# A two-layer decoder trunk on one core: smaller GpSimd pieces, a shorter group norm and a new order of the work between the chains of the RWKV scan

## The chip, the core and the metric

The kernel runs on one core of a Trainium2 chip. Its engines run side by side, each through its own fixed row of instructions, and wait for each other by semaphores: TensorE (PE in the profile; PEld is its loading of weights), VectorE (DVE), ScalarE (ACT), GpSimd (POOL) and SyncE (SP), which issues the transfers. The metric is the device time of one execution in microseconds, less being better.

## What is computed

Layer 0 has stick-breaking attention and a pooling mixer, layer 1 an RWKV-7 time mixing; a layer norm follows each. The sequence has 512 tokens, the model 2048 channels, all in float32. The change lies in layer 1. Its heart is a recurrence for each of 32 heads of 64 channels, followed by a group norm per head and a gate:

```
def step(state, inp):
    r_t, w_t, k_t, v_t, kk_t, a_t = inp
    sa = einsum('bhvk,bhk->bhv', state, -kk_t)
    state = state * w_t + sa[..., None] * (kk_t * a_t) + v_t[..., None] * k_t
    return state, einsum('bhvk,bhk->bhv', state, r_t)
...
mean = jnp.mean(o, axis=-1, keepdims=True)
var = jnp.mean(jnp.square(o - mean), axis=-1, keepdims=True)
o = ((o - mean) * lax.rsqrt(var + GN_EPS)).reshape(B_, S, D) * gn_w + gn_b
bonus = jnp.sum(r * k * r_k, axis=-1, keepdims=True) * v
o = (o + bonus.reshape(B_, S, D)) * jax.nn.silu(g)
return o @ w_o
```

## The kernel before

Matrix products are made in split precision: `split` (L135) writes a float32 tile as a high part (a cast on ACT, L137) and a low part (a subtraction, L138, on DVE, or on GpSimd where the caller says so), and `mm3` (L140) makes three matmuls of the parts. Layer 0, the projections of layer 1 (k, r, g) and the output projection are such products and are not touched.

`scan` (L827) takes the 32 heads in 16 pairs. For a pair the 512 tokens are cut into 8 chunks of 64, and within a chunk the recurrence is written as small matrix products. These functions make the parts of a pair:

- `vproj` (L857): the projection v, 16 blocks of 3 matmuls (L142 to L144, tile `vps`) in split precision. The weights come in units of four blocks; from the third pair on the low part of a unit, 128 x 512, is one GpSimd subtraction (`wlo`, L138).
- `gprod` (L876): loads the pair's factors, makes the products `g` of keys and queries in two halves (L890), masks them on DVE into `Z` (L896), and transposes the keys into `BT` (L902, L903). Each half of `g` takes two PSUM banks of the pool `pa`, which has two buffers and also serves the transpositions.
- `vprep` (L906): the bonus term `bv` on GpSimd (L911) and v by token (`RS`, L918 to L921).
- `lanes` (L926): the inverse of the diagonal blocks of 16, on DVE. Four GpSimd instructions gather the blocks (`nd`, L931), DVE transposes them (`lt`, L936), then 15 steps of one product `pr` and one sum `uc` each follow (L943, L944). It ends in `U` (L958).
- `levels` (L962): joins the blocks of 16 to 64 by four products on PE: `q1`, `c1` (added into `U` on DVE, L994, and transposed into `UT`, L996), `q2` (which reads `UT`) and `c2` (added into `U`, L1007).
- `chain` (L1010): the recurrence over the chunks, in three steps a chunk. In the first, PE makes `xo` (L1025 with the state `M`, L1028), and DVE and ACT copy it to `xs` (L1032, L1033). In the second, PE makes `sa` from `xs` and `U` (L1036), and DVE copies it to `RS` (L1037). In the third, PE makes `s1` from `RS` (L1043), DVE updates `M` (L1052, L1054), PE completes `xo` (L1057) and ACT copies it to `O` (L1060).
- `post` (L1064): the group norm of the pair's `O` on DVE and ACT (L1072 to L1083, with `rsqrt_eps`, L201), its transposition `ot` on PE (L1087), bonus and gate.

The order of PE's instructions is the order of the code; those of the other engines are put in a row by the scheduler, the chains' first. The main loop (from L1208) makes rounds of 12 slots. In a round two chains go one step a slot each: the second half of pair p's (the older one) and the first half of pair p+1's (the younger one). So slots 0, 3, 6 and 9 hold first steps, 1, 4, 7 and 10 second steps, and 2, 5, 8 and 11 third steps. Behind the two chains' step a slot holds what fills PE until the next one. `plan` (L1144) gives each visit of a generator a due time, spread evenly over an interval of slots, and `slot` (L1148) takes visits in the order of their due times. The intervals stand in L31 and L32, counted from the beginning of the round two before the one in which the pair's chain starts: `GP` for gprod, `VJ` for vproj, `LA` for lanes, `LV` for levels, `VP` for vprep, and `PO` for post. From pair 13 on, units of the output projection's weights and its first matmuls (`y`) fill in.

Of the kernel before, what the change touches and what calls it, by code (L numbers as in the profile page):

```python
# [8 lines left out]
F32 = mybir.dt.float32  # L9
# [20 lines left out]

PO, LA, VP, LV, GP, VJ = (13.5, 20), (8, 15), (21.5, 25), (16, 24.5), (0.5, 9), (5.5, 17)  # L31
Q14, A13, B13, A14, B14, A15, B15, Q15 = (0, 3), (0.5, 5.5), (6, 12), (0, 10), (3, 12), (0, 9), (0.5, 11.5), (0, 11.5)  # L32


class Kernel:
# [98 lines left out]

    def split(self, hi, lo, src, eng=None):  # L135

        self.nc.scalar.copy(hi, src)  # L137
        (eng or self.nc.vector).tensor_sub(lo, src, hi.bitcast(F32))  # L138

# [60 lines left out]

    def rsqrt_eps(self, pool, v, eps, n, name):  # L201
# [5 lines left out]
        nc.vector.tensor_scalar(hx, v, eps, -0.5, ALU.add, ALU.mult)  # L207
        nc.vector.reciprocal(sd, sd)
# [618 lines left out]
    def scan(self, ctx, xv, first, mp, ld, ar_d, bk_d, bc_d, g_d, m_d):  # L827
# [29 lines left out]
        def vproj(p):  # L857
# [18 lines left out]
        def gprod(p):  # L876
# [5 lines left out]
            nc.sync.dma_start(BK.rearrange("p a b -> p (a b)"), bk_d[p])  # L882
            yield

            Z = s["Z"] = [st.tile([P, 8, P], F32, tag=f"Z{h}", name=f"Z{h}", bufs=4) for h in range(2)]
            for b in range(2):
# [10 lines left out]
                yield  # L897
            BT = s["BT"] = st.tile([P, 8, P], F32, tag="BT", name="BT")
            for b in range(2):
                g = aux("bt")  # L900
                for c in range(4):
                    nc.tensor.transpose(g[:, c * P:(c + 1) * P], BK[:, 4 * b + c, :], self.ident)  # L902
                nc.scalar.copy(BT[:, 4 * b:4 * b + 4, :], g.rearrange("p (c n) -> p c n", c=4))  # L903
                yield

        def vprep(p):  # L906
# [3 lines left out]
            nc.sync.dma_start(bv, bc_d[p])  # L910
            nc.gpsimd.tensor_mul(bv, s["vT"], bv)  # L911

# [151 lines left out]
        def post(p):  # L1064
# [7 lines left out]
            nc.vector.tensor_reduce(sm, O, AX.X, ALU.add)  # L1072
            nc.vector.tensor_scalar(sm, sm, 1.0 / 64, None, ALU.mult)
# [6 lines left out]
            nc.vector.tensor_scalar(sm, sm, 1.0 / 64, None, ALU.mult)  # L1080
            rs = self.rsqrt_eps(tp, sm, GN_EPS, 8, "gn")
            yield
# [23 lines left out]
        def units(*ks):  # L1106
            for k in ks:
                tag = "AR,Z0,Z1,AR,Z0,Z1,BT,RS,AR,Z0,Z1,BT,RS,BK,AR,Z0".split(",")[k]
                pool = ld if tag in ("AR", "BK") else st
                w = pool.tile([P, 2, S], F32R, tag=tag, name="wo", bufs=1 if k == 13 else 4 if tag[-1] in "R01" and tag != "RS" else 3)  # L1110
                raw = self.wp.tile([P, S], F32, tag="wraw", name="wraw", bufs=3)
# [47 lines left out]
        def hurry(g):  # L1159
            while True:  # L1160
# [3 lines left out]
                yield  # L1164

        def plan_pair(base, q, skip=0):

            gp = gprod(q)
            next(gp)
            plan(base, gp, 6, *GP)  # L1170
            plan(base, hurry(lanes(q)) if q == 15 else lanes(q), 18, *LA)
            plan(base, hurry(levels(q)) if q == 15 else levels(q), 5, *LV)
# [6 lines left out]
        for q in range(3):  # L1179
            next(v)  # L1180
        run(gp)
        la = lanes(0)
        for q in range(16):
            next(la)
            if q % 2:
                next(v, None)
        g1, v = gprod(1), vproj(1)
        next(g1)
        run(la)
        for q in range(6):  # L1190
            next(g1)
            if q % 2:
                next(v)
        run(vprep(0))
        la, l0 = lanes(1), levels(0)
        for q in range(10):
            if q % 2 == 0:
                next(l0, None)
            if q < 6:
                next(la)  # L1200
            if q % 2:
                next(v)
        run(l0)
        plan(-12, la, 12, 12, LA[1])
        plan(-12, levels(1), 5, *LV)
        plan(-12, vprep(1), 2, *VP)
        A = None
# [111 lines left out]
```

## Time and profile before

| | |
|---|---|
| median of 3 runs | 2119.38 us (2112.89 to 2120.28) |
| the profiled execution | 2116.03 us, span 2114.3 us |
| mean granted clock of TensorE | 0.99 |
| scan: `vps` matmuls | 1401.4 to 1876.6 us |
| scan: `xo` matmuls | 1442.7 to 1942.4 us |
| `wlo` on GpSimd in the scan | 56 instructions, 74.6 us |
| `pr` (L943) of 128 x 81 on DVE | 14 instructions, mean 711 ns |

The profile is of one execution. A busy time is the union of the instructions' times on an engine; matmuls are pipelined and overlap, so a busy PE may still be waiting. In a row of the timeline stand the start, the length, the engine, the line, the operation, the tiles written and read, the shape of the array for matmuls (rows x columns), the shapes, and how many instructions are merged; in brackets stands the idle time before, with what ended it. A matmul of two float32 operands appears as two instructions. A row of the waits has the total in us, the number and the longest. In a group's row stand its busy time in us and the mean of one in ns, then the engine's idle time before it.

### The profile page before, as it was taken

How to read it: one execution, taken by the hardware profiler on the slowest of the kernel's cores; microseconds unless marked ns; L12 is line 12 of the kernel's file. 1: busy time of each engine (PE TensorE's matmuls, PEld its weight loads, DVE VectorE, ACT ScalarE, POOL GpSimd, SP SyncE). 2: the span in 40 equal slices, each digit the busy share in tenths (PEclk: the TensorE clock that was granted, in tenths of full speed). 3: DMA queues.
4: the chain of work that ended last, by engine and by line, in shares of the span. 5: the costliest groups of instructions: out<-in, count | busy, mean ns of one | idle time of the engine just before them, and what ended most of it. 6: DMA issues, size and time to landing. Idle time of an engine off the chain costs nothing. (4 is left out here: it accounts for less than half of the span.)

```text
span 2114.3 us, 33769 instructions
## 1 busy us (share of the span) xinstructions
PE 2032.7 (96%) x13139; PEld 1648.2 (78%) x13139; DVE 1295.1 (61%) x2557; ACT 956.5 (45%) x1663; POOL 250.1 (12%) x334
## 2 busy tenths in 40 slices
PE   8999999999999998999999999999999999989996
PEld 7888888888887897777788888877677676666786
DVE  5334344444433358656866776577888988886336
ACT  3345445333221138544654654455555555564211
POOL 0000000000000000233000000013333333310003
PEclk9999999999999999999999999999999999999998
DMA  5222222233333353565365556632232332232733
GB/s 192 91 79 80 80 80 65 85 95 105 100 102 117 111 176 111 157 179 173 110 210 192 197 173 217 202 120 62 91 101 81 96 106 89 85 115 95 235 105 114
DMA packets 214031, 262.97 MB, mean 124 GB/s; under 512 B 15768, under 2 KB 161776, under 8 KB 213104
## 3 DMA queue, kind: packets, MB, share of 16 engines
q1 hardware_dynamic: 213872, 260.83, 38.4%
q8 instruction: 103, 1.69, 0.3%
q14 instruction: 56, 0.46, 0.1%
HBM read 214.32 MB, written 46.47 MB: 123 GB/s over the span
## 5 line engine op out<-in xcount | busy, mean ns | idle before, releaser
L138 DVE TENSOR_TENSOR wlo<-wraw,whi 128x1024 fp32r<-128x1024 f32 (+1 forms) x268 | 313.8, 1175 | 475.9 <-ACT whi L137 464.6
L137 ACT CAST whi<-wraw 128x1024 fp32r<-128x1024 f32 (+1 forms) x324 | 302.9, 938 | 565.3 <-PE ga L143 327.0
L142 PE MATMUL ga<-mx,whi 128*128 128x512 f32 x768 | 299.9, 391 | 3.2 <-ACT mx L137 3.2
L142 PE MATMUL ga<-x,whi 128*128 128x512 f32 x768 | 300.9, 392 | 0.1
L143 PE MATMUL ga<-mx,whi 128*128 128x512 f32 x768 | 300.4, 391 | 0.0
L144 PE MATMUL ga<-mx,wlo 128*128 128x512 f32 x768 | 300.1, 391 | 0.0
L144 PE MATMUL ga<-x,wlo 128*128 128x512 f32 x768 | 299.5, 390 | 0.5 <-DVE wlo L138 0.5
L143 PE MATMUL ga<-x,whi 128*128 128x512 f32 x768 | 299.2, 390 | 0.0
L488 PE MATMUL gb<-whi,mixed 128*128 128x512 f32 (+1 forms) x576 | 198.0, 344 | 3.8 <-DVE s L439 3.8
L490 PE MATMUL gb<-wlo,mixed 128*128 128x512 f32 (+1 forms) x576 | 197.6, 344 | 3.1 <-DVE wlo L138 3.1
L489 PE MATMUL gb<-whi,mixed 128*128 128x512 f32 (+1 forms) x576 | 197.6, 343 | 0.0
L142 PEld LDWEIGHTS ga<-mx,whi 128*128 128x128 f32 x768 | 144.8, 189 | 36.1 <-ACT mx L137 3.6
L143 PEld LDWEIGHTS ga<-mx,whi 128*128 128x128 f32 x768 | 144.7, 188 | 31.5 <-DVE mx L138 0.6
L144 PEld LDWEIGHTS ga<-mx,wlo 128*128 128x128 f32 x768 | 144.8, 188 | 30.6
L144 PEld LDWEIGHTS ga<-x,wlo 128*128 128x128 f32 x768 | 144.2, 188 | 31.2 <-DVE wlo L138 1.0
L142 PEld LDWEIGHTS ga<-x,whi 128*128 128x128 f32 x768 | 144.3, 188 | 29.6 <-ACT whi L137 0.4
L143 PEld LDWEIGHTS ga<-x,whi 128*128 128x128 f32 x768 | 144.3, 188 | 29.1
L488 PEld LDWEIGHTS gb<-whi,mixed 128*128 128x128 f32 x576 | 109.8, 191 | 17.9 <-DVE s L439 5.4
L490 PEld LDWEIGHTS gb<-wlo,mixed 128*128 128x128 f32 x576 | 109.9, 191 | 16.8 <-DVE wlo L138 4.3
L489 PEld LDWEIGHTS gb<-whi,mixed 128*128 128x128 f32 x576 | 109.8, 191 | 12.4
L142 PE MATMUL vps<-mx,whi 128*128 128x512 f32 x256 | 113.8, 445 | 0.0
L138 POOL TENSOR_TENSOR wlo<-wraw,whi 128x512 fp32r<-128x512 f32 x56 | 74.6, 1332 | 257.0 <-ACT whi L137 234.8
(330 smaller groups left out, 3374.8 us busy)
## 6 DMA issues: line engine op xcount, KB each, us to landing
wraw<-in_ev_w_in SPq DMA_DIRECT2D x96, 512.0 KB, 3.6
wraw<-in_ev_w_out SPq DMA_DIRECT2D x32, 512.0 KB, 3.6
wraw<-in_od_w_k SPq DMA_DIRECT2D x32, 512.0 KB, 4.9
wraw<-in_od_w_r SPq DMA_DIRECT2D x32, 512.0 KB, 3.5
wraw<-in_od_w_g SPq DMA_DIRECT2D x32, 512.0 KB, 3.7
wraw<-in_od_w_v SPq DMA_DIRECT2D x64, 256.0 KB, 2.8
ar_d<-pAR SPq DMA_DIRECT2D x16, 512.0 KB, 2.6
bk_d<-pBK SPq DMA_DIRECT2D x16, 512.0 KB, 3.2
```

Of the source, the lines that this page charges most:

```text
L137: self.nc.scalar.copy(hi, src)
L138: (eng or self.nc.vector).tensor_sub(lo, src, hi.bitcast(F32))
L142: mm(ps, ah, bh, start=start, stop=False)
L143: mm(ps, ah, bl, start=False, stop=False)
L144: mm(ps, al, bh, start=False, stop=stop)
L488: mm(ps, ah, bh, start=start, stop=False)
L489: mm(ps, al, bh, start=False, stop=False)
L490: mm(ps, ah, bl, start=False, stop=stop)
```

## The change

The diff has three parts.

1. The GpSimd instructions of `vproj` and `vprep` are cut: the low part of a weight unit is made in four subtractions of 128 x 128, and `bv` in four products of 128 x 128.
2. In the group norm two scalings by 1/64 on DVE (L1073, L1080) are folded into their neighbours, and `hx` (L207) goes from DVE to ACT where it has eight columns.
3. `vproj` yields after each block, not after each second one. `gprod` makes `BT` ahead of `Z`, with four buffers of `BT`. The even intervals are replaced by due times of single visits (`at_`), except for post and lanes, and the interval of lanes is 4.5 to 17 where it was 8 to 15.

```diff
-PO, LA, VP, LV, GP, VJ = (13.5, 20), (8, 15), (21.5, 25), (16, 24.5), (0.5, 9), (5.5, 17)
+PO, LA = (13.5, 20), (4.5, 17)
...
-    def split(self, hi, lo, src, eng=None):
+    def split(self, hi, lo, src, eng=None, parts=1):
         self.nc.scalar.copy(hi, src)
-        (eng or self.nc.vector).tensor_sub(lo, src, hi.bitcast(F32))
+        n = src.shape[1] // parts
+        for q in range(parts):
+            sl = slice(q * n, q * n + n)
+            (eng or self.nc.vector).tensor_sub(lo[:, sl], src[:, sl], hi[:, sl].bitcast(F32))
...
-        self.split(hi, lo, raw, eng)
+        self.split(hi, lo, raw, eng, a if eng else 1)
...
-        nc.scalar.activation(sd, v, AF.Sqrt, bias=self.eps[eps])
-        nc.vector.tensor_scalar(hx, v, eps, -0.5, ALU.add, ALU.mult)
+        nc.scalar.activation(sd, v, AF.Sqrt, bias=self.eps[eps], scale=scale)
+        if n == 1:
+            nc.vector.tensor_scalar(hx, v, eps, -0.5, ALU.add, ALU.mult)
+        else:
+            nc.scalar.activation(hx, v, AF.Copy, bias=-0.5 * eps, scale=-0.5 * scale)
...
-                if k % 2 and k < NK - 1:
+                if k < NK - 1:
                     yield
...
-            nc.gpsimd.tensor_mul(bv, s["vT"], bv)
+            for q in range(4):
+                nc.gpsimd.tensor_mul(bv[:, q * P:q * P + P], s["vT"][:, q * P:q * P + P], bv[:, q * P:q * P + P])
...
-            nc.vector.tensor_scalar(sm, sm, 1.0 / 64, None, ALU.mult)
             yield
-            nc.vector.tensor_sub(O, O, bc(sm))
+            nc.vector.scalar_tensor_tensor(O, bc(sm), -1.0 / 64, O, ALU.mult, ALU.add)
...
-            nc.vector.tensor_scalar(sm, sm, 1.0 / 64, None, ALU.mult)
-            rs = self.rsqrt_eps(tp, sm, GN_EPS, 8, "gn")
+            rs = self.rsqrt_eps(tp, sm, GN_EPS, 8, "gn", 1.0 / 64)
...
+        def at_(base, g, *where):
+            todo.extend((base + x, len(todo), g) for x in where)
...
-            plan(base, gp, 6, *GP)
+            at_(base, gp, 1.6, 1.7, 3.1, 3.2, 4.1, 4.2)
...
-            plan(base, vproj(q), 8, *VJ)
-            plan(base, vprep(q), 2, *VP)
+            at_(base, vproj(q), *[x + 0.1 * n + 0.1 for x, m in ((5, 3), (7, 2), (8, 3), (11, 3), (13, 2), (14, 3)) for n in range(m)])
+            at_(base, vprep(q), 17.4, 19.5)
```

`levels` gets the due times 17.5, 18.1, 21.1, 22.1 and 24.1. In the steady rounds the work behind the chains' steps on PE is then this (v 6 stands for six matmuls of `vps`, `g` and `bt` for a half or the whole of their instructions):

| slot | step of the chains | before | after |
|---|---|---|---|
| 0 | first | a quarter of g, v 6 | c2 |
| 1 | second | a quarter of g | v 6, bt |
| 2 | third | v 6 | v 9 |
| 3 | first | a quarter of g, v 6 | half of g |
| 4 | second | a quarter of g | half of g |
| 5 | third | v 6, q1, ot | v 9, ot |
| 6 | first | half of bt, v 6 | q1 |
| 7 | second | c1, half of bt | v 6, vt |
| 8 | third | v 6 | v 9 |
| 9 | first | q2, v 6 | c1 |
| 10 | second | c2 | q2 |
| 11 | third | vt, v 6 | v 9 |

The first place is PE around the second steps of slots 7 (before) and 10 (after). Line numbers after the change are some 7 higher: L1043 is `sa`, L998 `c1`, L988 `q2` and `c2`, L1050 `s1`. Before:

```order
L1036 MATMUL sa<-xs_10939,U 64x128
L1036 MATMUL sa<-xs_10940,U 64x128
L991 MATMUL c_13649<-U,q1z 48x32 x16
L902 MATMUL bt<-ident,BK 128x128 x4
L1043 MATMUL s_13676<-RS,BT 64x64 x2
```

After, in slots 9 and 10:

```order
L998 MATMUL c_13368<-U,q1z 48x32 x16
L1043 MATMUL sa<-xs_10940,U 64x128
L1043 MATMUL sa<-xs_10939,U 64x128
L988 MATMUL q_13399<-UT,N_13242 32x32
L988 MATMUL q_13399<-UT,Z_12668 32x32
```

Before, two slots lie between `c1` and `q2`, with `s1`, `xo` and a run of `vps` in them; after, only the two `sa`. On DVE the same place after the change reads as follows (L1039 is the copy `xs`, L1044 the copy `RS`, L1001 the addition of `c1`, L1003 the transposition that `q2` reads, L950 and L951 the lanes of another pair):

```order
L1039 COPY xs_10940<-xo 64x64
L1039 COPY xs_10939<-xo 64x64
L950 TENSOR_TENSOR pr<-uc,la 128x10x10
L951 TENSOR_REDUCE uc<-pr 128x10
L1044 COPY RS<-sa 64x128 x2
L1001 TENSOR_TENSOR U<-U,c_14276 48x16x16 x2
L950 TENSOR_TENSOR pr<-uc,la 128x11x11
L1003 STREAM_TRANSPOSE UT<-U 128x256
```

Both `RS` and both additions stand ahead of `UT`.

The second place is PE in slots 0 and 1 before and 3 and 4 after, at the products `g`. Before:

```order
L890 MATMUL g<-AR,BK 128x128 x4
L142 MATMUL vps<-mx,whi 128x512
L143 MATMUL vps<-mx,whi 128x512
L144 MATMUL vps<-mx,wlo 128x512
L142 MATMUL vps<-mx,whi 128x512
L143 MATMUL vps<-mx,whi 128x512
L144 MATMUL vps<-mx,wlo 128x512
L1036 MATMUL sa<-xs_10940,U 64x128
L1036 MATMUL sa<-xs_10939,U 64x128
L890 MATMUL g<-AR,BK 128x128 x4
```

After (L903 is `g`):

```order
L903 MATMUL g<-AR,BK 128x128 x8
L1043 MATMUL sa<-xs_10939,U 64x128
L1043 MATMUL sa<-xs_10940,U 64x128
L903 MATMUL g<-AR,BK 128x128 x8
L1050 MATMUL s_13638<-RS,BT 64x64 x2
```

The two halves of `g`, which share two banks, now have only the two `sa` between them.

The third place is DVE in slots 0 and 1 after the change, where `c2` is added into `U` (L1014). The younger chain's first `sa` reads this `U`:

```order
L1039 COPY xs_10940<-xo 64x64
L1039 COPY xs_10939<-xo 64x64
L951 TENSOR_REDUCE uc<-pr 128x14
L1014 TENSOR_TENSOR U<-U,c_13925 32x8x32
L1044 COPY RS<-sa 64x128
L1014 TENSOR_TENSOR U<-U,c_13925 32x8x32
L950 TENSOR_TENSOR pr<-uc,la 128x15x15
L1085 TENSOR_REDUCE gs<-gsq 128x8
L1044 COPY RS<-sa 64x128
```

Before, the same additions (L1007) stand a slot earlier, around an update of `M`:

```order
L943 TENSOR_TENSOR pr<-uc,la 128x9x9
L1007 TENSOR_TENSOR U<-U,c_13341 32x8x32
L1052 SCALAR_TENSOR_TENSOR M_10942<-s_13360,pcs,m_13363 64x64 x2
L1007 TENSOR_TENSOR U<-U,c_13341 32x8x32
L944 TENSOR_REDUCE uc<-pr 128x9
```

The copy of the older chain's `RS` now stands between the two additions, and that of the younger behind both.

More of the change, by code (lines that the diff above doesn't have):

```diff
@@ L199, in rsqrt, with rsqrt_eps @@
         return y
-    def rsqrt_eps(self, pool, v, eps, n, name):
+    def rsqrt_eps(self, pool, v, eps, n, name, scale=1.0):
         nc = self.nc
@@ L883, in gprod @@
             yield
+            BT = s["BT"] = st.tile([P, 8, P], F32, tag="BT", name="BT", bufs=4)
+            for b in range(2):
+                g = aux("bt")
+                for c in range(4):
+                    nc.tensor.transpose(g[:, c * P:(c + 1) * P], BK[:, 4 * b + c, :], self.ident)
+                nc.scalar.copy(BT[:, 4 * b:4 * b + 4, :], g.rearrange("p (c n) -> p c n", c=4))
+                yield
             Z = s["Z"] = [st.tile([P, 8, P], F32, tag=f"Z{h}", name=f"Z{h}", bufs=4) for h in range(2)]
@@ L897, in gprod @@
                 yield
[L898 to L904, printed above, removed]
         def vprep(p):
@@ L1109, in units @@
                 pool = ld if tag in ("AR", "BK") else st
-                w = pool.tile([P, 2, S], F32R, tag=tag, name="wo", bufs=1 if k == 13 else 4 if tag[-1] in "R01" and tag != "RS" else 3)
+                w = pool.tile([P, 2, S], F32R, tag=tag, name="wo", bufs=1 if k == 13 else 3 if tag == "RS" else 4)
                 raw = self.wp.tile([P, S], F32, tag="wraw", name="wraw", bufs=3)
@@ L1184, in scan @@
             next(la)
-            if q % 2:
-                next(v, None)
+            next(v, None)
         g1, v = gprod(1), vproj(1)
@@ L1191, in scan @@
             next(g1)
-            if q % 2:
-                next(v)
+            next(v)
         run(vprep(0))
@@ L1200, in scan @@
                 next(la)
-            if q % 2:
-                next(v)
+            next(v)
         run(l0)
         plan(-12, la, 12, 12, LA[1])
-        plan(-12, levels(1), 5, *LV)
-        plan(-12, vprep(1), 2, *VP)
+        at_(-12, levels(1), 17.5, 18.1, 21.1, 22.1, 24.1)
+        at_(-12, vprep(1), 17.4, 19.5)
         A = None
```

6 lines of the change are left out of this document (3 added, 3 removed).

## The prediction, made before the changed kernel was run

> **What bounds the kernel now.** I read the page first, then the stages, then the waits inside the one stage that the diff touches, the scan (about 1,430 to 1,945 us).
>
> ```profile
> span 2114.3 us, 33769 instructions
> PE 2032.7 (96%) x13139; PEld 1648.2 (78%) x13139; DVE 1295.1 (61%) x2557; ACT 956.5 (45%) x1663; POOL 250.1 (12%) x334
> ```
> ```profile
> 1700.00:1800.00 100.00, 93.40 (x1182) 69.53 (x1178) 88.70 (x283) 55.00 (x140) 32.82 (x32) 0.98 0.35 106
> ```
>
> Columns of the stage row: length, then PE, PEld, DVE, ACT and POOL busy, then the granted clock. In the scan PE is busy 93.4 of 100 us and DVE 88.7. PE runs its instructions in one fixed row, so the scan lasts as long as PE works or waits. The chain that ended last gives the length of one pair, since the same instruction comes back in it every second pair:
>
> ```profile
> 1619.81 1.09 DVE rshgn L207
> ```
> ```profile
> 1744.32 1.09 DVE rshgn L207
> ```
>
> 124.5 us for four pairs: 31.1 us a pair of twelve slots. What PE visibly waits for in the scan:
>
> ```profile
> PE s L1043 <- DVE RS L1037: 22.9, 28, 1.7
> PE ot L1087 <- DVE O L1083: 4.0, 3, 2.8
> PE c L981 <- ACT q L1002: 2.6, 6, 1.0
> PE sa L1036 <- ACT xs L1033: 2.5, 7, 0.5
> PE xo L1025 <- DVE M L1054: 1.7, 4, 1.2
> ```
>
> One wait leads: PE's `s1` for the copy `RS`. The timeline shows where it comes from:
>
> ```profile
> 1647.81 0.17 DVE L1073 TENSOR_SCALAR gs<-gs 128x8 f32<-128x8 f32 x1
> ...
> 1650.56 1.28 POOL L138 TENSOR_TENSOR wlo<-wraw,whi 128x512 fp32r<-128x512 f32 x1 [4.06 <-ACT whi L137]
> 1650.64 1.23 DVE L1080 TENSOR_SCALAR gs<-gs 128x8 f32<-128x8 f32 x1
> ...
> 1652.82 0.66 PE L1043 MATMUL s<-RS,BT 128*64 128x64 f32 x8 [1.73 <-DVE RS L1037]
> ```
>
> The same scaling of eight numbers takes 0.17 us alone and 1.23 us beside a GpSimd subtraction that began 0.08 us before it: DVE stood still until GpSimd was done, `RS` behind it came late, and PE lost 1.73 us.
>
> **The change part by part.** The sum is made against the profiled execution, 2116.0 us (span 2114.3 and 1.7 around it), 3.4 below the median of 2119.38 and inside the runs shown.
>
> ```profile
> L138 POOL TENSOR_TENSOR wlo<-wraw,whi 128x512 fp32r<-128x512 f32 x56 | 74.6, 1332 | 257.0 <-ACT whi L137 234.8 <-DVE RS L1037 16.4 <-PE c L981 5.8
> L931 POOL TENSOR_TENSOR nd<-Z,md 32x256 f32<-32x256 f32 x56 | 40.9, 731 | 21.5 <-DVE Z L896 19.5
> ```
> ```profile
> L207 DVE TENSOR_SCALAR rshgn<-gs 128x8 f32<-128x8 f32 x15 | 7.0, 469 | 0.1
> L1080 DVE TENSOR_SCALAR gs<-gs 128x8 f32<-128x8 f32 x15 | 6.7, 448 | 0.1
> ```
>
> *GpSimd pieces and the group norm.* 256 elements cost 731 ns and 512 cost 1332, so a fixed part of about 130 ns: a piece of 128 is estimated at 130 + 1202/4 = 430 ns (bounds 333, a quarter, and 731). A DVE instruction that meets a piece should then stand for at most 0.43 us in place of 1.28, while a unit of weights takes 1.7 us in place of 1.3; PE asks for a unit a visit or more ahead, and POOL is busy 33 of 100 us, so that is hidden. The rows L207 and L1080 average 0.46 us where 0.17 is their size: they are the ones that are caught. Both leave DVE (the third, L1073, too); `hx` goes to ACT, busy 55 of 100 us. Of the 22.9 us I take 20 away (bounds 17 and 22.9).
>
> *Fewer changes of shape.* The order of PE's row before and after, gap by gap, has 30 changes of array shape a pair before and 24 after. One change costs this:
>
> ```profile
> 1647.42 0.92 PE L890 MATMUL g<-AR,BK 64*128 64x128 f32 x8
> 1648.27 0.50 PE L142 MATMUL vps<-mx,whi 128*128 128x512 f32 x1
> 1648.61 0.40 PE L143 MATMUL vps<-mx,whi 128*128 128x512 f32 x1
> 1648.84 0.39 PE L144 MATMUL vps<-mx,wlo 128*128 128x512 f32 x1
> ...
> 1649.53 0.39 PE L144 MATMUL vps<-mx,wlo 128*128 128x512 f32 x1
> 1649.85 0.60 PE L1036 MATMUL sa<-xs,U 128*64 128x128 f32 x4
> 1650.38 0.71 PE L890 MATMUL g<-AR,BK 64*128 64x128 f32 x8
> ...
> 1656.06 1.11 PE L890 MATMUL g<-AR,BK 64*128 64x128 f32 x8
> ...
> 1659.05 0.71 PE L890 MATMUL g<-AR,BK 64*128 64x128 f32 x8
> ```
>
> Inside a run a matmul starts 0.23 us after the last; the first gap is 0.34, and the exit 0.32: about 0.1 us at each end. Six changes by 0.1 by 14 pairs: -8 us (bounds -5 and -12).
>
> *g in two runs.* Four runs of eight took 0.92, 0.71, 1.11 and 0.71 us in this pair, 3.45; sixteen in one go took 1.16 in the row quoted further down, so two take 2.32. Of the 1.13 between them about half is the latency of the last matmul of two runs fewer, which the next run covers; -0.6 a pair is left, -8 us over 14 pairs (bounds -4 and -10).
>
> *Longer runs of v.* `v` comes after the third step of a slot triple in runs of nine, 2.3 us, where six gave 1.6. That covers the updates of `M`: the 1.7 us of `xo` waiting for `M` go, and waits inside a run that the list doesn't show; an estimate of -5 us (bounds -2 and -8). `c2` follows its `q2` by two slots with a run of v between: -2.5 us.
>
> Together -43.5 us. Now what is late next, since what was put after one step was taken from behind another. Three places in PE's row have a DVE product with no work of PE ahead of it:
>
> ```profile
> L896 DVE TENSOR_TENSOR Z<-g,mk 128x512 f32<-128x512 f32 x56 | 38.4, 686 | 1.5 <-PE g L890 0.4
> L1037 DVE COPY RS<-sa 64x128 f32<-64x128 f32 x128 | 37.0, 289 | 12.1 <-PE sa L1036 8.3
> L1032 DVE COPY xs<-xo 64x64 f32<-64x64 f32 x128 | 28.0, 219 | 11.8 <-PE xo L1028 8.6
> L1007 DVE TENSOR_TENSOR U<-U,c 32x256 f32<-32x256 f32 x31 | 12.6, 408 | 1.1 <-PE c L981 0.8
> ```
> ```profile
> L996 DVE STREAM_TRANSPOSE UT<-U 128x256 f32<-128x256 f32 x15 | 6.7, 445 | 0.4
> ```
>
> *First, `q2` behind `sa` (slots 9 and 10).* `c1`, `sa`, `sa`, `q2` stand next to each other. `q2` reads `UT`, and on DVE the row runs `xs`, `RS`, `RS`, the two additions into `U`, one lane step, `UT`. From the result of `sa` that is 0.29 + 0.29 + 0.41 (once or twice, as the order varies) + 0.445, so 1.4 to 1.8 us and the lane step. I take 1.6 us, 15 times: +24 (bounds 1.2 and 2.1). Behind `q2` on PE are the `s1` of both chains, the second `xo` and nine matmuls of v; all stand.
>
> *Second, the second half of `g` behind the first (slots 3 and 4).* The pool of these banks has two buffers, and each half takes both. The prologue of before does just this, back to back:
>
> ```profile
> 1405.53 1.16 PE L890 MATMUL g<-AR,BK 64*128 64x128 f32 x16
> 1407.47 1.75 PE L890 MATMUL g<-AR,BK 64*128 64x128 f32 x16 [0.78 <-DVE Z L896]
> ```
>
> 0.78 us idle and 0.59 us of stretching, 1.37. In the new order two `RS` (0.58) stand between the two `Z` on DVE, and the two `sa` (about 0.4 us of PE) lie in the gap: 1.5 us. I take 1.4, 14 times: +20 (bounds 1.0 and 1.7). Behind it stand `s1` and v again.
>
> *Third, `sa` behind `U` (slots 0 and 1).*
>
> ```profile
> 1643.67 0.69 PE L981 MATMUL c<-U,q 32*32 32x32 f32 x32 [0.33 <-ACT q L1002]
> ```
>
> The last step of the levels, `c2`, now comes in the first slot of the chain that needs it. After its 0.69 us DVE adds (0.41), copies the other chain's `RS` (0.29), adds again (0.41); then the younger chain's `sa` may start. PE has one `sa` to do meanwhile. 0.9 us, 15 times: +13.5 (bounds 0.5 and 1.6).
>
> *Fourth, the `xs` copies.* After the first step of a triple PE had six matmuls of v or more; now it has `c2`, `g`, `q1` or `c1`, 0.7 to 1.1 us. The copies take one DVE instruction (0.22), one on ACT of similar size, the matmul's own 0.2 and the hand-overs, 0.8 if nothing stands before them. With `lt`'s wait for GpSimd ahead of them in one slot I take 0.4 us a pair: +6 (bounds 0 and 14).
>
> The waits add 63.5 and the rest takes 43.5 away: +20. The lanes, spread over twelve slots where seven held them, are the same instructions; they cost DVE nothing more. The prologue has the same matmuls in finer steps, the tail only a fourth buffer for `BT`, the loads of `ar_d`, `bk_d` and `g_d` keep their places on SP, and `bc_d` comes four slots earlier; all at nothing, since 35% of the DMA engines' time is used and PE waited for no transfer in the rows above. 2116.0 + 20 = 2136.
>
> **The rivals.** *Faster: relief wins.* DVE gets its blocked time back, so its products come early, and each new wait is at its lower bound: 15 x 1.2 + 14 x 1.0 + 15 x 0.5 = 39.5. With the removals at their upper bounds (22.9 + 12 + 10 + 8 + 2.6 = 55.5) that is 2116 - 16 = 2100. It decides from the point at which the three new waits together fall below 3.0 us a pair (43.5 / 14.5). For it: DVE at 88.7 of 100 us is often what they queue behind, and `RS` and `xs` go first. Against it: the additions and the transposition are whole DVE instructions with sizes that no relief shortens.
>
> *No change: shapes cost more.* If a change costs 0.3 us (0.1 on each side and 0.1 of entry), six a pair save 25 us and not 8: 2136 - 17 = 2119. The page "TensorEngine Tiling (Array Packing)" of the Trainium skill, section "Tiling Modes", says that a change of tiling mode drains TensorE. That rule speaks for this rival. Against it: the quoted gaps show 0.1 us a side at a run of v, and four `sa` with the change to `g` behind them took 0.53 us in all (1649.85 to 1650.38).
>
> *Slower still: pieces hold DVE as long as one.* If four pieces in a row keep DVE out from the first to the last, only the three instructions that left DVE help: of caught time in L207 and L1080, (0.469 + 0.448 - 0.34) x 15 = 9 us. The gain is 9 in place of 20: 2147. Against it: the caught instruction above ended at 1651.87 us, 0.03 after the GpSimd one, so it was let in at once.
>
> The page "SBUF — State Buffer" of the Trainium skill, section "Who interferes with whom", says that whichever of DVE and GpSimd starts first holds the shared ports for the whole instruction. By that rule the next instruction to start after a piece is the DVE one that stands waiting, and this rival would come out at the forecast's 2136; the 0.03 us agree with it, but no run here yet shows several pieces in a row.
>
> **How the numbers follow.** The forecast, three waits against the relief, 0.50 (its own range 2122 to 2150). Relief wins 0.20; shapes 0.18; pieces 0.12. Measurements of this kernel tell about 0.5%, 10.6 us, from no change, so "same" is 2109 to 2130. The forecast puts 0.42 in slower and 0.08 in same; relief 0.17 in faster and 0.03 in same; shapes 0.14 in same and 0.03 in faster, 0.01 in slower; pieces 0.12 in slower. Faster 0.20, same 0.25, slower 0.55. With every cost at its upper bound and every gain at its lower the time is near 2180; that and the outer part of the faster case are left out: 2102 to 2156.
>
> **What would show it.** In the waits of PE after: `s1` for `RS` down from 22.9 to under 6 us, apart from what slot 4 adds; new rows of `q2` for `UT` near 24 us, `g` for `Z` near 20, `sa` for `U` near 13. In the rows of DVE no 128x8 instruction above 0.3 us. A pair in the chain that ended last 32 to 33 us long. A pair below 31 us, with the three new rows under 40 us together, would prove the sum wrong; `s1` for `RS` still at 20 us would prove the pieces wrong.

## The result, and the profile after

The changed kernel took 2184.36 us (median of 4 runs, 2180.64 to 2189.04), the kernel before, on the same chip and in the same job, 2117.52 us (4 runs). The ratio is 1.0319, with a 95% interval of 1.0289 to 1.0349: 3.2% slower. The forecast said slower, but by 20 us; it is 67 us, and the time lies above the range.

The head of the page of after (its execution took 2180.64 us), and the stage row of the scan, with the columns of the row shown of before:

```profile
span 2178.9 us, 33990 instructions
PE 2053.0 (94%) x13139; PEld 1678.9 (77%) x13139; DVE 1280.7 (59%) x2509; ACT 955.2 (44%) x1679; POOL 284.9 (13%) x550
```
```profile
1700.00:1800.00 100.00, 86.36 (x1035) 67.63 (x1031) 74.85 (x240) 48.75 (x128) 35.56 (x71) 0.91 0.26 80
```

PE has as many instructions as before (x13139). In 100 us of the scan it is busy 86.4 us where it was busy 93.4, and the granted clock is 0.91 where it was 0.98. DVE falls from 88.7 to 74.9 us: it is not the bound. PE waits more, and while it works it is slower.

What PE waited for in the scan (1430 to 2010 us) of after:

```profile
PE q L988 <- DVE UT L1003: 30.8, 16, 3.0
PE g L903 <- DVE Z L909: 17.0, 28, 0.8
PE sa L1043 <- DVE U L1014: 16.5, 14, 2.1
PE sa L1043 <- ACT xs L1040: 15.5, 32, 1.5
...
PE s L1050 <- DVE RS L1044: 0.2, 1, 0.2
```

The wait that the change was to remove is gone: 22.9 us before, 0.2 now. The four that the prediction named stand in its place, 79.8 us together. The list, with small rows, adds up to 81.5 us.

That is not all. The timeline of PE at slots 8 to 11 of one pair of after, columns start, length, instruction, idle time before it and its releaser (the instructions of `q2`, all on line 988, are left out but for the first):

```profile
1705.78 0.40 PE L146 MATMUL vps<-mx,whi 128*128 128x512 f32 x1
1706.01 0.39 PE L147 MATMUL vps<-mx,wlo 128*128 128x512 f32 x1
...
1709.78 0.69 PE L1043 MATMUL sa<-xs,U 128*64 128x128 f32 x4 [0.35 <-ACT xs L1040]
1712.37 0.18 PE L988 MATMUL q<-UT,Z 32*32 32x32 f32 x1 [1.90 <-DVE UT L1003]
...
1714.76 0.63 PE L146 MATMUL vps<-mx,whi 128*128 128x512 f32 x1
1715.19 0.63 PE L147 MATMUL vps<-mx,wlo 128*128 128x512 f32 x1
```

Ahead of the wait, matmuls of v start 0.23 us apart (1705.78, 1706.01); behind it the same two lines start 0.43 us apart (1714.76, 1715.19). The stretch cut into pieces of 3.41 us shows why. Columns: piece, its length, busy time of PE, PEld, DVE, ACT and POOL, then the granted clock:

```profile
1705.70:1709.10 3.40, 3.40 (x51) 2.68 (x51) 2.98 (x14) 1.98 (x5) 2.84 (x7) 1.00 0.60 180
1709.10:1712.50 3.40, 1.15 (x27) 0.76 (x23) 3.17 (x12) 0.41 (x2) 0.95 (x3) 0.99 0.72 230
1712.50:1715.90 3.40, 3.40 (x48) 2.93 (x46) 2.44 (x8) 2.27 (x6) 0.95 (x1) 0.50 0.01 2
1715.90:1719.30 3.40, 3.40 (x18) 2.31 (x17) 0.98 (x3) 0.63 (x1) 0.00 (x0) 0.50 0.00 0
1719.30:1722.70 3.40, 2.41 (x44) 1.79 (x41) 3.12 (x10) 0.56 (x3) 0.00 (x0) 1.00 0.02 5
```

In the second piece PE works for 1.15 of 3.40 us. Through the next two the clock is half, although PE has work in every microsecond of them. Between 1430 and 2010 us the clock's own record of after has 19 such drops, 92.2 us of half clock; before has three, 13.7 us.

The page "TensorE: Matmul & The Clock Gate" of the Trainium skill, section "HAM oscillation — how this bites in real kernels", gives as the rule that idle gaps of TensorE longer than about 3.4 us bring the half clock. The trace shows it behind a gap of 1.90 us with 0.35 us before it: here the drop went with the idle part of a piece of 3.41 us, not with one gap of that length (the counts stand in the last section).

For the comparisons below, one measure serves all kernels: ten pairs of the scan, from the third copy of `vT` (L879) to the thirteenth. In the kernels of the ledger further down these hold the same PE instructions (x3598 to x3602). Before, then after:

```profile
1475.60:1784.57 308.97, 288.20 (x3598) 214.19 (x3598) 273.05 (x857) 169.21 (x429) 104.36 (x100) 0.99 0.30 93
```
```profile
1477.16:1835.55 358.39, 306.87 (x3600) 240.38 (x3598) 262.80 (x828) 169.01 (x441) 127.75 (x250) 0.91 0.26 80
```

A pair went from 30.90 us (28.82 busy and 2.08 idle) to 35.84 us (30.69 busy and 5.15 idle).

### The profile page after: what moved, and what is told of

It is laid out like the page before. It is cut to its first block, busy times and chain, and to the rows that moved or that the text cites. A ratio compares the mean times of both kernels' runs of the same rounds, so it can differ in the third digit from the quotient of the medians.

```text
span 2178.9 us, 33990 instructions
## 1 busy us (share of the span) xinstructions
PE 2053.0 (94%) x13139; PEld 1678.9 (77%) x13139; DVE 1280.7 (59%) x2509; ACT 955.2 (44%) x1679; POOL 284.9 (13%) x550
## 4 chain that ended last, share of the span: by engine, by line
PE 78%; DVE 13%; DMA 3%; ACT 2%; issue 2%; POOL 1%; SPq 0%; DVEq 0%; ACTq 0%; POOLq 0%
PE ga L145 15%; PE ga L147 15%; PE ga L146 15%; PE gb L494 4%; PE gb L496 4%; PE gb L495 4%; PE vps L145 3%; PE vps L146 2%; PE vps L147 2%; DVE Z L909 1%; DVE pr L950 1%; PE g L903 1%; PE inc L359 1%; DVE uc L951 1%; PE xo L1032 1%
## 5 line engine op out<-in xcount | busy, mean ns | idle before, releaser
L141 POOL TENSOR_TENSOR wlo<-wraw,whi 128x128 fp32r<-128x128 f32 x224 | 101.4, 483 | 215.5 <-ACT whi L137 215.3
L145 PE MATMUL vps<-mx,whi 128*128 128x512 f32 x256 | 121.9, 476 | 0.5 <-ACT vT L879 0.5
```

The costliest lines, as they stand in the source:

```text
L141: (eng or self.nc.vector).tensor_sub(lo[:, sl], src[:, sl], hi[:, sl].bitcast(F32))
L145: mm(ps, ah, bh, start=start, stop=False)
```

## The experiments

Jobs ran on different chips, so times are compared through the ratio to the kernel before of the same job. "+20 us" below is the ratio less 1, times the 2117.5 us of before.

### The parts alone, and two repairs

The first four kernels asked which part loses, and whether each wait can be repaired where it stands. My theory then was that of the prediction: three waits, each with its own place and price.

`pieces` is the kernel before with only the GpSimd instructions cut in four:

```
-        (eng or self.nc.vector).tensor_sub(lo, src, hi.bitcast(F32))
+        n = src.shape[1] // parts
+        for q in range(parts):
+            sl = slice(q * n, q * n + n)
+            (eng or self.nc.vector).tensor_sub(lo[:, sl], src[:, sl], hi[:, sl].bitcast(F32))
...
-            nc.gpsimd.tensor_mul(bv, s["vT"], bv)
+            for q in range(4):
+                nc.gpsimd.tensor_mul(bv[:, q * P:q * P + P], s["vT"][:, q * P:q * P + P], bv[:, q * P:q * P + P])
```

> The old order with the GpSimd pieces alone. Theory (the new order's waits made it slow, the pieces are a gain): PE's wait of s1 for RS falls from 22.9 us to 5 to 10, the time by 12 to 18 us to about 2102. Rival (the pieces themselves cost: a unit of weights takes 4 x 0.48 = 1.9 us of GpSimd in place of 1.3, and DVE is held as long): the wait stays near 20 us and the time is 2117 or more.

Measured: 2093.92 us, ratio 0.9905 (0.9889 to 0.9922), -20 us: a little more than the 12 to 18 expected, although the wait fell to 11.6 us and not to 5 to 10. Its rows for PE's wait, for the pieces on GpSimd, and for the two small DVE instructions that had been caught:

```profile
PE s L1047 <- DVE RS L1041: 11.6, 24, 0.8
```
```profile
L141 POOL TENSOR_TENSOR wlo<-wraw,whi 128x128 fp32r<-128x128 f32 x224 | 100.8, 481 | 216.8 <-ACT whi L137 203.9 <-DVE RS L1041 13.0
```
```profile
L1084 DVE TENSOR_SCALAR gs<-gs 128x8 f32<-128x8 f32 x16 | 2.9, 181 | 0.1
L210 DVE TENSOR_SCALAR rshgn<-gs 128x8 f32<-128x8 f32 x16 | 2.8, 174 | 0.1
```

A piece takes 481 ns and not the 430 of the estimate, so a unit costs GpSimd 1.92 us instead of 1.33; nobody waits for that. The instructions that were caught at a mean of 0.46 us are at their own size again, though they are still on DVE. Most of them meet no piece any more. Two do, and they show that DVE is let in behind one piece, not behind the whole unit; one of them:

```profile
1495.54 1.87 POOL L141 TENSOR_TENSOR wlo<-wraw,whi 128x128 fp32r<-128x128 f32 x4 [3.62 <-ACT whi L137]
```
```profile
1496.17 0.42 DVE L1084 TENSOR_SCALAR gs<-gs 128x8 f32<-128x8 f32 x1
```

The scaling ended at 1496.59 us, the four pieces at 1497.41. The other one (L210, at 1555.16 us) took 0.32 us and ended 1.08 us ahead of its unit.

`pieces_gn` adds the shorter group norm:

```
-            nc.vector.tensor_scalar(sm, sm, 1.0 / 64, None, ALU.mult)
...
-            nc.vector.tensor_sub(O, O, bc(sm))
+            nc.vector.scalar_tensor_tensor(O, bc(sm), -1.0 / 64, O, ALU.mult, ALU.add)
...
+            nc.scalar.activation(hx, v, AF.Copy, bias=-0.5 * eps, scale=-0.5 * scale)
```

> The old order with the pieces and the shorter group norm. Theory: the wait of s1 for RS under 5 us, the time 18 to 25 us below before, about 2096. Rival: as the pieces alone or no gain at all, 2110 to 2120.

Measured: 2093.51 us, ratio 0.9904 (0.9889 to 0.9918). It adds nothing that can be measured, and `s1` still waits 10.3 us for `RS`, where under 5 was expected. Its ten pairs, 29.27 us each, 28.21 busy and 1.06 idle:

```profile
1472.40:1765.14 292.74, 282.13 (x3600) 211.57 (x3600) 253.39 (x827) 169.12 (x438) 126.50 (x250) 1.00 0.31 98
```

So everything that was lost, 88 us from here to after, was lost by the reordering: 6.57 us a pair, 4.09 of them idle and 2.48 more busy time for the same instructions. By the clock's record the ten pairs of after hold 64.9 us of half clock, those of `pieces_gn` none.

`levels_apart` is after with a slot and more between `c1` and `q2`:

```
-at_(base, hurry(levels(q)) if q == 15 else levels(q), 17.5, 18.1, 21.1, 22.1, 24.1)
+at_(base, hurry(levels(q)) if q == 15 else levels(q), 17.5, 18.1, 19.4, 21.1, 23.9)
```

> The changed kernel with the levels' products spread again (c1 in slot 7, q2 in slot 9, c2 in slot 11). Theory: the waits of q2 for UT (30.8 us) and of sa for U (16.5) go, and with them the half clock behind slot 10 (some 20 us); slots 9, 10 and 0 lose what filled them, for which xs and RS are waited for by some 15 us more: about 2130. Rival (the longer runs of v and the lanes spread over twelve slots made it slow): 2165 or more.

Measured: 2168.56 us, ratio 1.0258 (1.0243 to 1.0274), nearer to the rival than to the 2130 of the theory. Its waits:

```profile
PE g L903 <- DVE Z L909: 30.9, 27, 2.2
PE sa L1043 <- ACT xs L1040: 21.2, 42, 1.0
PE s L1050 <- DVE RS L1044: 8.3, 16, 1.0
...
PE q L988 <- DVE UT L1003: 0.9, 1, 0.9
```

The two waits aimed at are gone (`q2` for `UT` 30.8 to 0.9; `sa` for `U` 16.5 to 1.3), and 28 of those 45 us are back at `g`, `xs` and `RS`.

`g_apart` is after with three slots between the halves of `g`, and the lanes, v's first run and vprep moved to make room:

```
-at_(base, gp, 1.6, 1.7, 3.1, 3.2, 4.1, 4.2)
+at_(base, gp, 1.6, 1.7, 3.1, 3.2, 7.1, 7.2)
...
-PO, LA = (13.5, 20), (4.5, 17)
+PO, LA = (13.5, 20), (7.6, 17)
...
-((5, 3), (7, 2), (8, 3)
+((4, 2), (5, 3), (8, 3)
...
-at_(base, vprep(q), 17.4, 19.5)
+at_(base, vprep(q), 17.4, 20.5)
```

> The changed kernel with the second half of g in slot 7, a run of six v in slot 4 in its place, lanes and the transposition of v after it. Theory: the wait of g for Z (17.0 us) goes, and the half clock that follows slot 4 in part of the pairs (some 8 us): about 2160. Rival (the waits only move, since DVE's copies are late anyway): 2175 to 2190.

Measured: 2194.88 us, ratio 1.0385 (1.0362 to 1.0407), slower than after itself and over both expectations:

```profile
PE sa L1043 <- ACT xs L1040: 41.2, 25, 3.9
PE sa L1043 <- DVE U L1014: 15.9, 14, 1.5
PE q L988 <- DVE uc L951: 15.0, 8, 2.0
PE q L988 <- DVE pr L950: 11.1, 6, 2.1
```

The wait at `g` is gone from the list, `xs` and the squeezed lanes cost more than it did, and the half clock in the scan grew from 92 to 142 us. The run moves four things at once, so it does not price the place of `g` alone. But the theory of three separate waits fell with these two runs: a wait that is repaired by moving something else is paid elsewhere. Two questions were left. What do the moves cost apart, and what makes them cost more together? And does the half clock cost time by itself, or does it only fill time that other engines need anyway?

### The moves apart and together

`p_g` is `pieces_gn` with gprod alone in the new order: the code for `BT` stands ahead of `Z` as in the diff, and

```
-            plan(base, gp, 6, *GP)
+            at_(base, gp, 1.6, 1.7, 3.1, 3.2, 4.1, 4.2)
```

> The two parts that gain (2093.5 us) and, of the reordering, only gprod: transpositions of B first, then g in two visits of two runs each (slots 1, 3 and 4), with Z multiplied after each half. Theory: the second half of g waits for Z 17 to 20 us in all (0.6 us each, 28 times), g's fewer visits give back up to 8 us, and since these waits are under a microsecond the clock drops only after some: 2100 to 2112. Rival (fewer visits pay, and the wait is one that the chain would have had at its own steps): 2085 to 2093.

Measured: 2100.50 us, ratio 0.9930 (0.9908 to 0.9953); 5.5 us over `pieces_gn`. Its ten pairs:

```profile
1476.91:1773.15 296.24, 281.71 (x3602) 212.25 (x3604) 255.62 (x830) 168.16 (x438) 127.51 (x250) 0.99 0.31 97
```

Idle 1.45 a pair (+0.39), busy 28.17 (-0.04). `g` waited 10.9 us for `Z`, less than the 17 expected: in PE's row a run of six of v still stands between the halves. And the saving that fewer visits were to bring does not show in PE's busy time.

`p_levels3` is `pieces_gn` with only the levels moved:

```
-            plan(base, hurry(levels(q)) if q == 15 else levels(q), 5, *LV)
+            at_(base, hurry(levels(q)) if q == 15 else levels(q), 16, 18.1, 21.1, 22.1, 23.5)
```

> The two parts that gain (pieces, shorter group norm: 2093.5 us) and, of the reordering, only the places of the levels: q1 due at 18.1, c1 at 21.1, q2 at 22.1, c2 at 23.5, so that q2 stands about one slot behind c1. v, g, the transpositions, vprep and the lanes keep the places of before. Theory (two costs of each wait): q2 waits for UT 1.6 to 1.9 us in each of 16 pairs, 25 to 30 us, and a half clock follows that costs up to 1.7 us a pair where a run of v stands behind it; the shapes give back some 3 us: 2130 to 2145. Rival (the wait alone counts): 2115 to 2122. Rival (the levels' places matter only together with the lanes' and v's): within 8 us of 2093.

Measured: 2104.76 us, ratio 0.9949 (0.9930 to 0.9968); 9.5 us over `pieces_gn`. The theory's 2130 missed; the last of the rivals, that the levels' places matter only together with v's, is the nearest. `q2` waited 6.2 us for `UT`, in place of 25 to 30: with v where it was before, a run of it stands between `c1` and `q2` (slot 9). What grew beside it is the wait of `s1` for `RS`, from 10.3 to 20.5 us.

`p_v` is `pieces_gn` with only v in the new runs (vproj yields after each block, and the prologue steps it as after does):

```
-            plan(base, vproj(q), 8, *VJ)
+            at_(base, vproj(q), *[x + 0.1 * n + 0.1 for x, m in ((5, 3), (7, 2), (8, 3), (11, 3), (13, 2), (14, 3)) for n in range(m)])
```

> The two parts that gain (2093.5 us) and, of the reordering, only the runs of v: 3, 2, 3, 3, 2, 3 blocks behind six slots and none in slots 3, 4, 9, 10 and 12, where before eight slots held two each. Theory (what is taken from the bare slots uncovers the copies of xs, 15.5 us in the changed kernel against 2.9): sa waits for xs 8 to 15 us in all, a half clock follows part of them, longer runs give back 2 to 5: 2100 to 2112. Rival (longer runs pay and ScalarE has the copies done): 2086 to 2093.

Measured: 2122.01 us, ratio 1.0034 (1.0022 to 1.0046); 27.5 us over `pieces_gn`. This move alone takes back more than the pieces gain, and costs more than either side expected (2112 at most). The leading wait of `p_v`, and its ten pairs:

```profile
PE sa L1043 <- ACT xs L1040: 30.4, 53, 1.6
```
```profile
1475.64:1786.63 310.99, 287.65 (x3600) 217.91 (x3598) 258.53 (x826) 169.22 (x439) 128.59 (x250) 0.99 0.29 92
```

`sa` waits 30.4 us for `xs`, where it waited 2.9 in `pieces_gn`: v had been the cover of those copies. A pair is 31.10 us, 2.33 idle. The whole list of waits grew by 15.9 of the 27.5 us (26.0 to 41.9), and ten us more of half clock would be some 3 (the price is found below). The other 8 show as longer busy time, 0.56 us a pair at a granted clock of 0.99; their cause stays open.

`p_vl` puts the last two edits together.

> The two parts that gain (2093.5 us), with v's new runs and the levels' new places together (c2 at 23.5); g, lanes and vprep as before. Alone the levels cost 11 us and v's runs 28 us. Theory (they meet in slots 9 and 10, which v leaves bare just as c1 and q2 move there, so the sum is more than the parts): q2 waits for UT over 15 us in all, half clocks follow, 2140 to 2160. Rival (the parts add): 2128 to 2136.

Measured: 2156.92 us, ratio 1.0199 (1.0178 to 1.0220); 62.5 us over `pieces_gn`, where the two alone add up to 37. The waits that lead, and the ten pairs:

```profile
PE q L988 <- DVE UT L1003: 29.8, 16, 3.0
PE sa L1043 <- ACT xs L1040: 21.7, 37, 1.6
```
```profile
1473.69:1814.77 341.08, 305.32 (x3600) 237.85 (x3598) 266.54 (x828) 170.42 (x442) 126.35 (x250) 0.90 0.27 84
```

The wait of `q2` is whole again (29.8 us), and the clock is 0.90. A pair has 2.52 us more idle time than in `pieces_gn`, and 2.32 us more busy time for the same instructions.

`v_back` is the reverse: after with v alone back at its due times of before.

```
-at_(base, vproj(q), *[x + 0.1 * n + 0.1 for x, m in ((5, 3), (7, 2), (8, 3), (11, 3), (13, 2), (14, 3)) for n in range(m)])
+at_(base, vproj(q), *[5.5 + 11.5 * n / 8 + x for n in range(8) for x in (0, 0.01)])
```

> The changed kernel with v alone put back to the due times of before: eight runs of two blocks, in slots 0, 2, 3, 5, 6, 8, 9 and 11 in place of 1, 2, 5, 7, 8 and 11. Levels, g, lanes and vprep stay where the change put them. A run now stands between c1 and q2 (slot 9), in slot 0 ahead of the younger chain's first steps, and between two halves of g (slot 3). Theory (the reordering loses because three of its moves meet: the levels, g and the copies xs all want the cover of v in slots that v has left): q2 for UT under 8 us, sa for xs under 6, g for Z under 12, few half clocks, time 2095 to 2125. Rival (each place costs its own: q2 a slot behind c1, g's halves too close, c2 beside the first steps): only the xs waits and a part of q2's go, 2150 to 2170.

Measured: 2112.99 us, ratio 1.0001 (0.9988 to 1.0015), 67 us under after, with levels, `g`, lanes and vprep left where the change put them. Its waits and its ten pairs:

```profile
PE s L1050 <- DVE RS L1044: 12.1, 22, 1.9
...
PE sa L1043 <- ACT xs L1040: 3.8, 11, 0.9
...
PE q L988 <- DVE UT L1003: 1.5, 1, 1.5
PE g L903 <- DVE Z L909: 0.8, 2, 0.4
```
```profile
1475.91:1778.53 302.62, 283.08 (x3599) 213.14 (x3598) 255.38 (x827) 170.36 (x438) 126.96 (x250) 0.99 0.30 95
```

Three of the four new waits are down to 6.1 us together, and the fourth, `sa` for `U`, is not in the list. The pair is 30.26 us, and nearly all of the half clock is gone (18.1 us of it in the scan, 92.2 in after). The rival, that each place has its own price, falls. What is left, 20.5 us over `pieces_gn`, belongs to levels, `g`, lanes and vprep together; lanes and vprep were not tried alone.

`c2_early` is after with `c2` due at 23.5 and not 24.1, behind slot 11:

```
-at_(base, hurry(levels(q)) if q == 15 else levels(q), 17.5, 18.1, 21.1, 22.1, 24.1)
+at_(base, hurry(levels(q)) if q == 15 else levels(q), 17.5, 18.1, 21.1, 22.1, 23.5)
```

> The changed kernel with one number of the levels changed: c2 due at 23.5 in place of 24.1, so that it stands behind slot 11 with the last run of v, and the addition to U comes a slot ahead of the younger chain's first sa. Theory (the wait of sa for U costs its 16.5 us and the half clocks behind it): that wait falls under 4 us, time 2160 to 2170. Rival (the lost time turns up at the next wait, xs or q2, since the two chains cannot go faster than their own steps): 2178 to 2186.

Measured: 2191.35 us, ratio 1.0359 (1.0337 to 1.0380); slower than after by 8 us, which neither side expected. The rival is the nearer:

```profile
PE q L988 <- DVE UT L1003: 29.6, 15, 3.0
PE sa L1043 <- ACT xs L1040: 28.9, 46, 1.4
PE g L903 <- DVE Z L909: 14.6, 22, 0.8
...
PE sa L1043 <- DVE U L1014: 0.4, 1, 0.4
```

The wait for `U` went from 16.5 to 0.4 us and the one for `xs` grew by 13.4: `c2` had been the only cover of `xs` in slot 0. The half clock in the scan grew from 92 to 127 us, while the list of waits got shorter, 78.0 us in place of 81.5: what made this kernel slower is not in that list. At the price found below, 0.30 to 0.35 us for each, 35 us more of half clock are 10 to 12 us.

### What the half clock costs

`fill_q2` is after with zeros multiplied into v's open bank where PE waits for `UT`, so that the idle time is filled and nothing is moved:

```
+        zt = tp.tile([P, 96], F32R, name="zt")
+        nc.vector.tensor_scalar(zt, self.ident[:, :96], 0.0, None, ALU.mult)
...
+            if cur[0] is not None:
+                for _ in range(8):
+                    mm(cur[0][:96], zt, xv[0][:, 0, :], start=False, stop=False)
             g = prod("q2", N, UT, 0, 32, 32)
```

> The changed kernel, with eight matmuls of zeros (96 columns of weights, 512 columns moving, adding nothing to v's open bank) put on TensorE just ahead of q2, where it waits 30.8 us in all for UT: idle time becomes work of the same length (8 x 0.23 us = 1.8 us a pair), and everything else stays. Theory (the idle time costs twice: by itself, and by the half clock that follows it): the wait of q2 for UT falls under 8 us, the rows of the run of v behind slot 10 start 0.23 us apart and not 0.43, the pair loses some 1.7 us, the time falls by 20 to 30 us to about 2160, and the scan's granted clock rises from 0.91 to 0.95 or more. Rival (the half clock has another cause, such as the load of TensorE as a whole, or costs nothing since other engines set the pair): the time stays at 2184 or goes up by what the matmuls overrun, to 2184 to 2195.

Measured: 2163.38 us, ratio 1.0230 (1.0207 to 1.0254), 19 us under after, with some 29 us of useless matmuls in it. The waits and the ten pairs (lines of this kernel stand 4 to 7 higher; 3683 instructions, 80 of them zeros):

```profile
PE sa L1050 <- DVE U L1021: 20.2, 14, 2.1
PE sa L1050 <- ACT xs L1047: 16.9, 30, 1.5
PE g L907 <- DVE Z L913: 16.8, 28, 0.8
PE q L992 <- DVE UT L1007: 2.4, 2, 1.5
```
```profile
1476.95:1817.67 340.72, 305.16 (x3683) 235.81 (x3680) 263.00 (x828) 169.19 (x442) 124.98 (x250) 0.97 0.26 84
```

A pair is 34.07 us, 30.52 of it busy. Without the zeros (8 x 0.23 = 1.84 us) the busy time is 28.68 where after has 30.69: the same instructions in 2.0 us less. Idle time fell by 1.6, about what the zeros took. So the gain lies in the busy time, and it goes with the clock: half clock in the scan went from 92.2 to 37.5 us. The price is 19 us for 54.6, 0.35 us for each.

`p_vl_fill` does the same to `p_vl`, where the wait of `q2` makes nearly all of the half clock.

> The kernel with v's new runs and the levels' new places (2156.9 us), with the eight matmuls of zeros ahead of q2, as in the changed kernel before. There they took 54.6 us of half clock out of the scan (92.2 to 37.5 us between 1430 and 2010 us) and the time fell by 21 us, 0.38 us for each. Theory (half clock behind the wait of q2 has a price of its own, in proportion to how long it lasts): nearly all of the 92.2 us of half clock here stands behind this one wait, so 14 to 25 us of it are left, and 67 to 78 us less at 0.38 us each give 25 to 30 us: 2127 to 2132. Rival (what the matmuls saved in the changed kernel came from something else in its slots, such as a later start of what stands behind them): 2145 to 2160.

Measured: 2136.52 us, ratio 1.0107 (1.0090 to 1.0124), 19.5 us under `p_vl`; half clock from 92.2 to 27.3 us. The ten pairs:

```profile
1476.39:1800.38 323.99, 307.47 (x3680) 233.81 (x3678) 266.57 (x828) 169.99 (x441) 126.37 (x250) 0.97 0.28 88
```

Less than the 25 to 30 us expected, but on the theory's side: 0.30 us for each microsecond of half clock. The page "TensorE: Matmul & The Clock Gate" of the Trainium skill, section "HAM oscillation — how this bites in real kernels", reckons half of the throttled time, 0.5 where it is half speed. The 0.30 and 0.35 lie under that. That waiting and hand-overs inside these stretches make the difference is likely, but was not measured.

### The ledger

| kernel | ratio to before | us against `pieces_gn` | a pair: busy + idle, us |
|---|---|---|---|
| before | 1 | +20 | 28.82 + 2.08 |
| `pieces_gn` | 0.9904 | 0 | 28.21 + 1.06 |
| `p_g` | 0.9930 | +5.5 | 28.17 + 1.45 |
| `p_v` | 1.0034 | +27.5 | 28.77 + 2.33 |
| `v_back` | 1.0001 | +20.5 | 28.31 + 1.95 |
| `p_vl` | 1.0199 | +62.5 | 30.53 + 3.58 |
| after | 1.0319 | +88 | 30.69 + 5.15 |

`pieces` and `pieces_gn` beat both kernels: 1.0% under before and 4% under after.

## Why the prediction was wrong, step by step

- **Pieces, -20 us: right in the sum, and half of it in the row that was named.** Alone they give 20 us (0.9905). `s1`'s wait for `RS` gives 11.3 of them (22.9 to 11.6 us); PE's busy time, which the sum did not have, fell by 0.51 us a pair (28.82 to 28.31), some 8 us in sixteen. The 0.2 us of after are not the pieces' doing alone: `p_levels3`, with the same pieces, waits 20.5 there. The rival that four pieces hold DVE as long as one fell: the caught rows went from 0.46 to 0.17 and 0.18 us. The rule from the page "SBUF — State Buffer" of the Trainium skill, section "Who interferes with whom", that the first of the two holds the ports for a whole instruction, agrees with the trace: the two scalings that met a piece in `pieces`, of 0.42 and 0.32 us, came in behind that one piece. The part of this term that I gave the group norm is nothing measurable.
- **PE's gains by shapes and by `g`, -16 us: not found.** In the busy time of a pair, `p_g` with `g` in two runs is 0.04 us better than `pieces_gn`, where I had taken 0.6. In `v_back`, which has every move but v's, it is 0.10 worse. The half microsecond between two runs of `g` that I called removable was not PE's to give back. The rival that a change of shape costs 0.3 us, and so gives 25 us back, is not borne out: with levels and `g` in the new order no gain in busy time showed. The 2.5 us for `c2` came: its wait for `q`, 2.6 us before, is in no row of after.
- **The three waits, +57.5 us: right in kind and not far off in size.** 24 for `q2`, 20 for `g` and 13.5 for `sa` at `U`; the profile has 30.8, 17.0 and 16.5.
- **The copies `xs`, +6 us: the place right, the size wrong.** 15.5 in after, 13.0 more than before, and 30.4 in `p_v`. The bounds, 0 to 14, counted one slot a pair; the cover had gone from several.
- **"Longer runs of v", -5 us: this step failed.** I priced the move of v by what its longer runs cover, and priced what v had left as three waits of other edits. The saving itself was there: from start to start, v's own matmuls took 12.58 us a pair in `p_v` and 12.99 in `pieces_gn` (576 of them in twelve pairs). But `p_v` shows that the move as a whole costs 27 us. `v_back` shows that undoing it takes 67 us off after. Levels and `g` in the same new places cost little as long as v stands between their halves: `p_levels3` +9.5, `p_g` +5.5. The waits were put to the wrong account, and so the sum treated as separate what hangs on one cover.
- **What the sum left out altogether: the half clock.** Each wait was counted as long as it lasts. Behind `q2`'s came up to 6.83 us at half clock, and the two fill kernels show that this has a price of its own. At 0.30 to 0.35 us for each of the 78.5 us of half clock that after has more than before, that is 24 to 27 us.

With these the sum closes: waits +75.8 (30.8 - 1.5, 17.0, 16.5 and 15.5 - 2.5), half clock +24 to +27, `RS` -22.7, and small waits of before that went (`ot`, `c`, `M`, 9.7 together) -10: +67 to +71, against 67 measured. The prediction had 63.5 for the waits, nothing for the clock, and 43.5 of relief where these rows have 32.7. That it closes so well is in part luck: reckoned from `pieces_gn` the same way, waits (26.0 to 81.5 us) and half clock give 79 to 83 of the 88 us, and the rest stays open, as in `p_v`. With every cost at its upper bound the prediction had 2180, near the measured time; since neither the half clock nor the shared cover is in that sum, this too is chance. Its warning sign, three new rows under 40 us with a pair under 31 us, did not come: the rows are 64.3 us together and the pair 35.8, so the miss lay on the other side.

## What to carry to other kernels

Work that fills an engine's waits is not free to move: before a filler is moved, list for each place that it leaves what is computed there by other engines, since every such place is a wait, and two edits that use the same filler can cost more together than apart. On a TensorE-bound stage price an idle stretch twice, by its length and by the slow clock behind it, and read the granted clock in pieces as short as the stall. When a change bundles a local repair with a reordering, time the repair alone: here it gives 1% by itself, and the bundle lost 3%.

## What the runs showed of the hardware

- The granted clock changes in steps of 3.41 us, and whether it drops went with how much of the step before PE was idle. In the fourteen kernels, of 2,145 steps at full clock between 1430 and 2010 us, those with under 1.0 us of idle time were never followed by half clock (0 of 1,935); those with 1.0 to 1.8 us were in 66 of 146 cases; those with 1.8 us and more in all 64. These are counts from the clock's record and PE's rows, worked out after the runs; no experiment varied the idle time in small steps. Two waits of under a microsecond in one step were enough: in after, 0.47 and 0.82 us at `g`.
- Half clock mostly lasted one step or two. How idle PE was before the drop does not tell which: with 1.8 us and more it was two steps in all 13 cases of `p_vl`, but one step in 6 of 11 of after. What PE did in the first step at half clock tells more. Where it was busy all through that step, half clock ended with it in 60 of 66 cases; where it was idle at all, half clock went on in 58 of 64. There are exceptions of both kinds: the drop of after shown above lasted two steps with PE busy all through the first, and five of `fill_q2` lasted one although PE had up to 0.41 us of idle time in it. Rows of one of these five:

```profile
1704.40:1707.80 3.40, 1.98 (x48) 1.30 (x46) 3.23 (x10) 1.48 (x6) 0.00 (x0) 1.00 0.00 0
1707.80:1711.20 3.40, 3.12 (x8) 2.34 (x9) 2.96 (x10) 1.52 (x3) 0.47 (x2) 0.50 0.00 0
1711.20:1714.60 3.40, 3.40 (x32) 2.77 (x32) 1.13 (x4) 2.64 (x7) 1.23 (x3) 1.00 0.29 81
```

- In `p_vl` a pair is 34.11 us long, ten steps of the clock within 0.1%, and the drops come every 34.13 us. Whether the pair locked on to the clock's steps, or met them by chance, was not tried.
- A GpSimd subtraction of 128x128 takes 481 ns and one of 128x512 takes 1332: by these two rows some 200 ns of an instruction do not depend on its length, where the prediction had 130.
